# Scores of two head pairs in one tick, and the last norm's operands loaded at the end: a hybrid decoder layer

## The chip, the cores and the metric

The kernel runs on one core of one Trainium2 chip. A core has five engines that work side by side: TensorE (PE; its weight loads are listed apart as PEld), VectorE (DVE), ScalarE (ACT), GpSimd (POOL) and SyncE (SP, which here only issues DMAs). The metric is device time in microseconds. A forecast is a time and the chances of faster, same or slower.

## What is computed

One layer, 256 tokens of width 2048, all in float32. A norm, one input projection, two groups of 16 heads of 64 (sliding-window attention with sinks and ALiBi, two key heads shared; forgetting attention, FoX, where a decay of the running sum of log f is added), a norm per group, an output projection, a norm and the residual; then a GeGLU channel mixer with a causal convolution of width 3 and again a norm and the residual.

```python
h = rmsnorm(x, pre_mix_g); proj = h @ w_in
o_a = swa_sink_attention(q_a, k_a, v_a, sinks)      # 16 heads, window 128, ALiBi
o_b = forgetting_attention(q_b, k_b, v_b, log_f)    # 16 heads
mix = concat(rmsnorm(o_a, grp_swa_g), rmsnorm(o_b, grp_fox_g)) @ w_out
x = x + rmsnorm(mix, post_mix_g)
u = causal_dwconv(rmsnorm(x, pre_ffn_g) @ w_up, conv_w, conv_b)
y = (gelu(gate(u)) * val(u)) @ w_down
out = x + rmsnorm(y, post_ffn_g)
```

## The kernel before, in words

**Products.** Every weight tile is split into a high part (`whi`, a cast on ScalarE) and a low part (`wlo`, raw minus high, on VectorE; lines 112 and 115 for the projections), and each product is done as high x high, high x low and low x high. Each part has five buffers, so ScalarE and VectorE can be some units ahead of TensorE, and each raw tile too, filled by SP.

**Ticks.** TensorE's instructions run in the order in which the code issues them. The projections call `tick()` at fixed places: eight times in one `proj_T` (256 output columns, 32 products of 512 columns and 32 of 256), behind three of four k-tiles in the V projection, once per six products in the output projection. `later(n, f)` has `f` issued at the n-th tick from now. In this way attention work is dropped between the products of the projections. ScalarE, VectorE, GpSimd and SP get their order from a scheduler during the attention; in the last stage it is the order of the code.

**Attention.** Heads go in pairs, and a group is two pairs whose q (for FoX also k) comes from one projection. `attend` registers four steps per pair: `tables` (GpSimd writes the bias table into tile `p`, two buffers; for FoX after a DMA of `cb`), `scores` (12 products on 64 rows each, line 475, into two banks of the ring "att", which has four; then on VectorE four passes of line 481 that add the table and take the maximum, on ScalarE four exponentials of line 493, on VectorE the reciprocal 497 and four scalings 500), `transposes` (six of `p`, line 510, into two banks, then split) and `pv` (the weighted values, lines 522 to 536, into one bank, then into `oT`). `stages(n)` gives the ticks of the last three: n, n + 6, n + 9; the tables come three ticks before n. Sliding-window pairs take n = 6 and 14 after their group's start, FoX pairs n = 3 and 11, in groups of 16 ticks. FoX keys are scaled on GpSimd (line 442) and split into `keys` (lines 312 and 313) before their scores.

**The end.** The down projection goes in two halves of 22 tiles of 128 hidden features, each in two column passes, with `sums` (of the tag "x") as an operand of the fast products. In the last pass the products of the last three units are held back for the end (`block(i)`), their weights being read from `rest`. Then for each token half: the sum of the last banks (`down`, 1097 and 1098, with the squares on ScalarE), times the gain vector `gbf` on GpSimd (`gain`, 1091), the rstd (`rstd_y`, a power on GpSimd, 1173), and `finish` (1177: y times rstd plus `x_back` on VectorE, and the store). GpSimd's order there is: gain of four 512-wide pieces, the rstd of the first token half, three and a half more, the second rstd, the last half piece. `gbf` is loaded when the second half's up projection is over; the two halves of `x_back` are loaded into `tb` and `extra`, buffers of the weight loads, when each is free.

Of the kernel before, what the change touches and what calls it, by code (L numbers as in the profile page):

```python
# [17 lines left out]
P = 128  # L18
S = 256
D = 2048  # L20
# [11 lines left out]
def hybrid_layer(ctx: ExitStack, tc: tile.TileContext, x, pre_mix_g, w_in, b_forget, sinks,  # L32
# [27 lines left out]
    def later(n, f):  # L60
        todo.setdefault(now[0] + n, []).append(f)
# [253 lines left out]
    with tc.tile_pool(name="mixp", bufs=1) as mp:  # L315
# [277 lines left out]

        def stages(n):
            return n, n + 6, n + 9

# [23 lines left out]
        for g in range(4):  # L620
            if g == 0:
                b2 = bq0
            else:
                b2 = [bank(), bank()]
                proj_T(w_in, g * 256, b2)
            for m in range(2):
                swa_pair(2 * g + m, q_pair(b2[m]), stages(6 + 8 * (2 * g + m) - 8 * g))

# [59 lines left out]
        for g in range(4):  # L688
            bq = [bank(), bank()]
            proj_T(w_in, 1280 + g * 256, bq)  # L690
            qs = [q_pair(b) for b in bq]
            bk = [bank(), bank()]
            proj_T(w_in, 2304 + g * 256, bk)
            for m in range(2):
                ki = (2 * g + m + 2) % NK
                k_pair(bk[m], ki)
                fox_pair(2 * g + m, qs[m], ki, stages(3 + 8 * m))


        later(stages(11)[2] + 4, lambda: group_rstd(1, rstd_b))  # L700
        mix_sb = main.tile([P, 2, D], F32, tag="y", name="mix_sb")
# [145 lines left out]
    with tc.tile_pool(name="ffn", bufs=1) as fp:  # L847
# [200 lines left out]
        ysq = [small.tile([P, 5], F32, tag=f"ysq{t}", bufs=1, name=f"ysq{t}") for t in range(2)]  # L1048
        gbf = None
        for half in range(2):  # L1050
# [4 lines left out]
            for g in range(FHALF // 2):  # L1055
# [32 lines left out]
            def gain(t, n, h=None, into=None):  # L1088
                cs = slice(0, 512) if h is None else slice(h * 256, h * 256 + 256)
                ys = y_sb[:, t, n * 512:(n + 1) * 512][:, cs]  # L1090
                pool.tensor_tensor(ys if into is None else into, ys,
                                   gbf[:, n * 512:(n + 1) * 512][:, cs], op=ALU.mult)

# [19 lines left out]
            for n in (0, 2):  # L1113
# [39 lines left out]
                for i in range(4):  # L1153
                    block(i)
                    t, c = divmod(i, 2)
                    if half:
                        down(t, n + c, late[i])
                    else:
                        dve.tensor_tensor(y_of(t, c), late[i], y_of(t, c), op=ALU.add)

        def before_last(t, n):
# [14 lines left out]
        def finish(t, cs, r, q, y=None):  # L1176
            dve.scalar_tensor_tensor(y_sb[:, t, cs], y_sb[:, t, cs] if y is None else y, r,
                                     x_back[t][:, cs], op0=ALU.mult, op1=ALU.add)
            q.dma_start(of[t * P:(t + 1) * P, cs], y_sb[:, t, cs])
# [3 lines left out]
                     mybir.EngineType.SP}))  # L1183
        x_back = [tb[:, 0:2, :].rearrange("p a c -> p (a c)"),
                  extra.rearrange("p a c -> p (a c)")]
        for t in range(2):
            sp.dma_start(x_back[t], x_dram[t * P:(t + 1) * P, :])
        gain(0, 0)
# [61 lines left out]
```

## Time and profile before

| | us |
|---|---|
| median of 3 runs | 1069.38 (1068.11 to 1071.11) |
| the profiled execution, its own time | 1067.23 |
| its span in the trace | 1065.5 |
| TensorE busy in the span | 1051.2 |
| VectorE, ScalarE, GpSimd busy | 843.8, 637.6, 225.9 |

The granted clock is 0.997 on average. Rows of the trace give the start in us from the span's beginning, the duration in us, engine, line, operation, written tile <- read tiles, shapes, a count and, in brackets, the idle time ahead and what ended it. "x2" behind a row means that two are merged into it. A busy TensorE may still go slowly: spacings of its products tell that.

### The profile page before, as it was taken

How to read it: one execution, taken by the hardware profiler on the slowest of the kernel's cores; microseconds unless marked ns; L12 is line 12 of the kernel's file. 1: busy time of each engine (PE TensorE's matmuls, PEld its weight loads, DVE VectorE, ACT ScalarE, POOL GpSimd, SP SyncE). 2: the span in 40 equal slices, each digit the busy share in tenths (PEclk: the TensorE clock that was granted, in tenths of full speed). 3: DMA queues.
4: the chain of work that ended last, by engine and by line, in shares of the span. 5: the costliest groups of instructions: out<-in, count | busy, mean ns of one | idle time of the engine just before them, and what ended most of it. 6: DMA issues, size and time to landing. Idle time of an engine off the chain costs nothing.

```text
span 1065.5 us, 16294 instructions
## 1 busy us (share of the span) xinstructions
PE 1051.2 (99%) x5890; PEld 913.3 (86%) x5890; DVE 843.8 (79%) x1369; ACT 637.6 (60%) x1096; POOL 225.9 (21%) x256
## 2 busy tenths in 40 slices
PE   9999999999999999999999999999999999999996
PEld 7889988887889988888888888888888888888885
DVE  5988877887567888687777989668778687789996
ACT  6766766666656766565555555446566565656561
POOL 4243343342022121121212000002112121200103
PEclk9999999999999999999999999999999999999998
DMA  8745656555783776665666565666566665666572
GB/s 289 209 119 171 180 164 205 170 150 158 294 259 106 257 225 190 198 196 165 214 182 195 181 225 191 223 189 192 181 198 196 192 188 182 196 215 206 188 250 86
DMA packets 154284, 207.08 MB, mean 194 GB/s; under 512 B 6844, under 2 KB 131036, under 8 KB 153180
## 3 DMA queue, kind: packets, MB, share of 16 engines
q1 hardware_dynamic: 153200, 203.37, 61.0%
q10 hardware_dynamic: 1004, 2.68, 0.6%
q8 instruction: 46, 0.75, 0.3%
q14 instruction: 34, 0.28, 0.1%
HBM read 201.68 MB, written 4.21 MB: 193 GB/s over the span
## 4 chain that ended last, share of the span: by engine, by line
PE 91%; DVE 4%; DMA 1%; POOL 1%; issue 1%; ACT 1%; SPq 0%; DVEq 0%; POOLq 0%; ACTq 0%
PE bank_acc L284 16%; PE bank_att L967 15%; PE bank_att L284 14%; PE bank_acc L309 12%; PE bank_acc L290 8%; PE bank_att L290 7%; PE bank_acc L253 7%; PE bank_acc L258 3%; PE bank_acc L967 3%; PE bank_att L475 1%; PE bank_att L510 1%; DVE wlo L115 1%; DVE wlo L313 1%; PE bank_acc L932 1%; DMA x_in<-in_x_dram 1%
## 5 line engine op out<-in xcount | busy, mean ns | idle before, releaser
L115 DVE TENSOR_TENSOR wlo<-raw,whi 128x1024 fp32r<-128x1024 f32 (+3 forms) x271 | 330.3, 1229 | 117.4 <-ACT whi L112 112.9
L112 ACT CAST whi<-raw 128x1024 fp32r<-128x1024 f32 (+3 forms) x270 | 273.3, 1029 | 124.8 <-issue 88.9
L899 POOL TENSOR_TENSOR room<-room,rowf 128x256 f32<-128x256 f32 x88 | 100.3, 1160 | 393.9 <-DVE room L898 392.0
L284 PE MATMUL bank_acc<-hT,whi 128*128 128x512 f32 x736 | 173.3, 390 | 0.0
L284 PEld LDWEIGHTS bank_acc<-hT,whi 128*128 128x128 f32 x736 | 136.4, 188 | 27.4
L967 PE MATMUL bank_att<-whi,G 128*128 128x512 f32 x488 | 156.1, 389 | 0.0
L284 PE MATMUL bank_att<-hT,whi 128*128 128x512 f32 x640 | 150.6, 390 | 0.0
L284 PEld LDWEIGHTS bank_att<-hT,whi 128*128 128x128 f32 x640 | 118.7, 188 | 23.9
L967 PEld LDWEIGHTS bank_att<-whi,G 128*128 128x128 f32 x488 | 91.6, 188 | 18.9
L967 PE MATMUL bank_att<-wlo,G 128*128 128x512 f32 x244 | 95.0, 389 | 0.4 <-DVE wlo L313 0.4
L290 PEld LDWEIGHTS bank_acc<-hT,wlo 128*128 128x128 f32 x736 | 89.3, 188 | 2.0
L290 PE MATMUL bank_acc<-hT,wlo 128*128 128x256 f32 x736 | 89.9, 279 | 0.0
L901 ACT ACTIVATE room<-room,cw 128x256 f32<-128x256 f32 x88 | 53.0, 602 | 60.6 <-POOL room L899 60.6
L253 PE MATMUL bank_acc<-hT,whi 128*128 128x512 f32 x352 | 89.2, 396 | 0.0
L309 PE MATMUL bank_acc<-whi,oT 128*128 128x512 f32 (+1 forms) x272 | 82.5, 380 | 0.0
L290 PEld LDWEIGHTS bank_att<-hT,wlo 128*128 128x128 f32 x640 | 77.6, 188 | 1.7
L290 PE MATMUL bank_att<-hT,wlo 128*128 128x256 f32 x640 | 77.9, 279 | 0.0
L903 DVE SCALAR_TENSOR_TENSOR room<-room,cw 128x256 f32<-128x256 f32 x88 | 62.4, 709 | 17.6 <-ACT room L901 17.3
L253 PEld LDWEIGHTS bank_acc<-hT,whi 128*128 128x128 f32 x352 | 63.0, 188 | 11.3
L313 DVE TENSOR_TENSOR wlo<-raw,whi 128x1024 fp32r<-128x1024 f32 (+1 forms) x56 | 61.3, 1118 | 13.4 <-ACT whi L312 13.4
L312 ACT CAST whi<-tb 128x1024 fp32r<-128x1024 f32 x42 | 44.0, 1050 | 43.4 <-PE bank_att L967 19.7
L312 ACT CAST whi<-raw 128x1024 fp32r<-128x1024 f32 (+1 forms) x56 | 52.4, 958 | 28.9 <-PE bank_att L967 22.3
(255 smaller groups left out, 1591.1 us busy)
## 6 DMA issues: line engine op xcount, KB each, us to landing
raw<-in_w_up_dram SPq DMA_DIRECT2D x176, 512.0 KB, 4.1
raw<-in_w_down_dram SPq DMA_DIRECT2D x58, 512.0 KB, 4.9
raw<-in_w_in_dram SPq DMA_DIRECT2D x51, 512.0 KB, 3.9
raw<-in_w_out_dram SPq DMA_DIRECT2D x32, 512.0 KB, 4.3
extra<-in_w_down_dram SPq DMA_DIRECT2D x20, 512.0 KB, 4.8
raw<-in_w_in_dram SPq DMA_DIRECT2D x16, 384.0 KB, 3.5
tb<-in_w_down_dram SPq DMA_DIRECT2D x10, 512.0 KB, 3.6
cb<-c_dram SPq DMA_DIRECT2D x8, 256.0 KB, 3.6
```

The source lines that it names most:

```text
L112: i1 = act.copy(hi[:, cs], raw[:, cs])
L115: i2 = dve.tensor_tensor(lo[:, cs], raw[:, cs], hi[:, cs].bitcast(F32), op=ALU.subtract)
L253: pe.matmul(b, parts[u][0][:, a, m * P:(m + 1) * P], hT[:, kt, :], start=(kt == 0), stop=(kt == KT - 1))
L284: pe.matmul(b, parts[u][0][:, a, m * P:(m + 1) * P], hT[:, kt, :], start=(kt == 0), stop=(kt == KT - 1))
L290: pe.matmul(b[:, 256:512], parts[u][1][:, a, m * P:(m + 1) * P], hT[:, kt, 0:256], start=False, stop=False)
L309: pe.matmul(b, a, r[:, cols], start=(first and i == 0), stop=(last and i == 2))
L312: act.copy(hi, src)
L313: dve.tensor_tensor(lo, src, hi.bitcast(F32), op=ALU.subtract)
L899: pool.tensor_tensor(u[:, 2:258], u[:, 2:258], rowf, op=ALU.mult)
L901: act.activation(y, u[:, 2:258], AF.Identity, bias=cw[:, 3, ch:ch + 1], scale=cw[:, 2, ch:ch + 1])
L903: dve.scalar_tensor_tensor(y, u[:, 1:257], cw[:, 1, ch:ch + 1], y, op0=ALU.mult, op1=ALU.add)
L967: pe.matmul(b[:, to] if to else b, a, r[:, cols], start=(first and i == 0), stop=(last and i == 2))
```

## The change

`stages` gets the pair's number m: both pairs of a group have their scores in one tick; the first keeps n, n + 6, n + 9, the second gets n, n + 9, n + 13. Sliding-window groups take n = 7 and FoX groups n = 6. `gbf` and `x_back` are allocated and loaded after all the weight loads: `x_back` as a tile of its own in the place of `sums`, `gbf` in the place of `extra`, and `rest` moves to the place of `hT`. The function `gain` moves, with the same content.

```diff
-        def stages(n):
-            return n, n + 6, n + 9
+        def stages(n, m):
+            return n, n + 6 + 3 * m, n + 9 + 4 * m
...
-                swa_pair(2 * g + m, q_pair(b2[m]), stages(6 + 8 * (2 * g + m) - 8 * g))
+                swa_pair(2 * g + m, q_pair(b2[m]), stages(7 + 8 * g, m))
...
-                fox_pair(2 * g + m, qs[m], ki, stages(3 + 8 * m))
+                fox_pair(2 * g + m, qs[m], ki, stages(6, m))
...
-        later(stages(11)[2] + 4, lambda: group_rstd(1, rstd_b))
+        later(stages(6, 1)[2] + 4, lambda: group_rstd(1, rstd_b))
...
-            if half == 1:
-                gbf = main.tile([P, 4 * D], F32, tag="hT", name="gbc_ffn")[:, 0:D]
-                sp.dma_start(gbf, post_ffn_g[0].partition_broadcast(P))
...
-                    rest = main.tile([P, 2, 2, UNIT], F32R, tag="x", name="rest")
+                    rest = main.tile([P, 2, 2, UNIT], F32R, tag="hT", name="rest")
...
-                                     x_back[t][:, cs], op0=ALU.mult, op1=ALU.add)
+                                     x_back[:, t, cs], op0=ALU.mult, op1=ALU.add)
...
-        x_back = [tb[:, 0:2, :].rearrange("p a c -> p (a c)"),
-                  extra.rearrange("p a c -> p (a c)")]
+        x_back = main.tile([P, 2, D], F32, tag="x", name="x_back")
         for t in range(2):
-            sp.dma_start(x_back[t], x_dram[t * P:(t + 1) * P, :])
+            sp.dma_start(x_back[:, t, :], x_dram[t * P:(t + 1) * P, :])
+        gbf = fp.tile([P, D], F32, tag="gbc", name="gbc_ffn")
+        sp.dma_start(gbf, post_ffn_g[0].partition_broadcast(P))
         gain(0, 0)
```

What this does to the order on the engines, at three places. TensorE at the scores of the first FoX group, before: one pair's twelve products stand among the low products (`wlo`) of the next q projection.

```order
L258 MATMUL bank_acc<-hT,wlo 128x256 x10
L475 MATMUL bank_att<-keys,qh 128x256 x2
L475 MATMUL bank_att<-keys,ql 128x256 x2
L475 MATMUL bank_att<-keys,qh 128x256 x2
L475 MATMUL bank_att<-keys,qh 128x128 x2
L475 MATMUL bank_att<-keys,ql 128x128 x2
L475 MATMUL bank_att<-keys,qh 128x128 x2
L258 MATMUL bank_acc<-hT,wlo 128x256 x6
L253 MATMUL bank_acc<-hT,whi 128x512 x16
```

TensorE at the same place in the changed kernel, from the first pair's last three rows on (its first three and the product rows ahead, `L253` x14, are left out): the second pair follows at once, and 2 high and 16 low products of the two units in use come behind.

```order
L475 MATMUL bank_att<-keys,qh 128x128 x2
L475 MATMUL bank_att<-keys,ql 128x128 x2
L475 MATMUL bank_att<-keys,qh 128x128 x2
L475 MATMUL bank_att<-keys,qh 128x256 x2
L475 MATMUL bank_att<-keys,ql 128x256 x2
L475 MATMUL bank_att<-keys,qh 128x256 x2
L475 MATMUL bank_att<-keys,qh 128x128 x2
L475 MATMUL bank_att<-keys,ql 128x128 x2
L475 MATMUL bank_att<-keys,qh 128x128 x2
L253 MATMUL bank_acc<-hT,whi 128x512 x2
L258 MATMUL bank_acc<-hT,wlo 128x256 x16
L253 MATMUL bank_acc<-hT,whi 128x512 x16
```

So the block has moved behind 6 low and 14 high products, and two blocks have become one. VectorE at the scores of the second FoX group (`p_2340` is the first pair's table, `nm` the maxima, `rs` the sums), before:

```order
L481 ISA p_2340,nm_2382<-bank_att_2368,p_2340 128x256
L481 ISA nm_2382 128x1
L481 ISA p_2340,nm_2382<-bank_att_2369,p_2340 128x256
L481 ISA nm_2382 128x1
L481 ISA p_2340,nm_2382<-bank_att_2368,p_2340 128x128
L481 ISA nm_2382 128x1
L481 ISA p_2340,nm_2382<-bank_att_2369,p_2340 128x128
L481 ISA nm_2382 128x1
L497 RECIPROCAL rs_2387<-rs_2387 128x4
L500 TENSOR_SCALAR p_2340<-p_2340,rs_2387 128x256 x2
L500 TENSOR_SCALAR p_2340<-p_2340,rs_2387 128x128 x2
L115 TENSOR_TENSOR wlo_2595<-raw_2592,whi_2594 128x1024
```

VectorE at that place in the changed kernel, behind the first pair's four passes (`p_2373`): the second pair's (`p_2383`) lie around the first pair's reciprocal and scaling, and then comes the next split.

```order
L481 ISA p_2383,nm_2468<-bank_att_2454,p_2383 128x256
L481 ISA nm_2468 128x1
L497 RECIPROCAL rs_2444<-rs_2444 128x4
L481 ISA p_2383,nm_2468<-bank_att_2455,p_2383 128x256
L481 ISA nm_2468 128x1
L500 TENSOR_SCALAR p_2373<-p_2373,rs_2444 128x256 x2
L500 TENSOR_SCALAR p_2373<-p_2373,rs_2444 128x128 x2
L481 ISA p_2383,nm_2468<-bank_att_2454,p_2383 128x128
L481 ISA nm_2468 128x1
L481 ISA p_2383,nm_2468<-bank_att_2455,p_2383 128x128
L481 ISA nm_2468 128x1
L115 TENSOR_TENSOR wlo_2586<-raw_2583,whi_2585 128x1024
```

So eight passes instead of four stand between two splits; ahead of them the splits `wlo_2522`, `wlo_2528` and `wlo_2580` are already done, and `wlo_2404` and `wlo_2410` are those in use. SP at the end, before:

```order
L69 DMA raw<-in_w_down_dram 128x1024 x3
L1187 DMA tb<-x_dram 128x2048
L69 DMA raw<-in_w_down_dram 128x1024
L1187 DMA extra<-x_dram 128x2048
L1179 DMA out_dram<-y_sb 128x512 x6
```

SP at the end in the changed kernel:

```order
L69 DMA raw<-in_w_down_dram 128x1024 x4
L1182 DMA x_back<-x_dram 128x2048 x2
L1184 DMA gbc_ffn<-in_post_ffn_g_dram 128x2048
L1175 DMA out_dram<-y_sb 128x512 x6
L1175 DMA out_dram<-y_sb 128x256
```

The last weight load no longer stands behind a load of x, and the gain vector comes third behind two of x, a megabyte each. GpSimd's order at the end stays as told above.

More of the change, by code (lines that the diff above doesn't have):

```diff
@@ L1048, in hybrid_layer @@
         ysq = [small.tile([P, 5], F32, tag=f"ysq{t}", bufs=1, name=f"ysq{t}") for t in range(2)]
-        gbf = None
         for half in range(2):
@@ L1083, in hybrid_layer @@
                     token_sums(sums[:, FAST.index(g), :], *ys)
-            if half == 1:
-                gbf = main.tile([P, 4 * D], F32, tag="hT", name="gbc_ffn")[:, 0:D]
-                sp.dma_start(gbf, post_ffn_g[0].partition_broadcast(P))
[L1088 to L1092, printed above, removed]
             def down(t, n, b, h=None):
@@ L1159, in hybrid_layer, with gain @@
                         dve.tensor_tensor(y_of(t, c), late[i], y_of(t, c), op=ALU.add)
+        def gain(t, n, h=None, into=None):
+            cs = slice(0, 512) if h is None else slice(h * 256, h * 256 + 256)
+            ys = y_sb[:, t, n * 512:(n + 1) * 512][:, cs]
+            pool.tensor_tensor(ys if into is None else into, ys,
+                               gbf[:, n * 512:(n + 1) * 512][:, cs], op=ALU.mult)
         def before_last(t, n):
```

## The prediction

> **What bounds the kernel.** I read the busy line of the page and the shares of the chain that ended last, then a table by stretch, then the order of time inside the stretches in which TensorE lost time.
>
> ```profile
> PE 1051.2 (99%) x5890; PEld 913.3 (86%) x5890; DVE 843.8 (79%) x1369; ACT 637.6 (60%) x1096; POOL 225.9 (21%) x256
> PE 91%; DVE 4%; DMA 1%; POOL 1%; issue 1%; ACT 1%; SPq 0%; DVEq 0%; POOLq 0%; ACTq 0%
> 150.00:175.00 25.00, 23.85 (x150) 20.59 (x148) 17.50 (x34) 14.05 (x28) 13.65 (x20) 1.00 0.64 203
> 225.00:250.00 25.00, 24.19 (x146) 20.37 (x145) 20.92 (x43) 15.23 (x37) 11.48 (x16) 1.00 0.53 150
> 1000.00:1050.00 50.00, 49.64 (x220) 40.73 (x219) 44.40 (x54) 26.91 (x33) 3.43 (x4) 1.00 0.53 179
> 1050.00:1065.50 15.50, 6.04 (x44) 5.56 (x42) 9.86 (x15) 1.74 (x6) 6.48 (x7) 0.81 0.37 135
> 363.81 3.63 PE bank_att L284 x16
> 367.44 3.73 PE bank_att L290 x32
> ```
>
> TensorE is the bound: 99% busy, 91% of the chain. (In the stretches the columns after the length are PE, PEld, DVE, ACT, POOL busy, then the granted clock, the DMA share and GB/s.) A 512-column product costs 3.63/16 = 0.227 us, a 256-column one 3.73/32 = 0.117 us, and the change adds or removes none. So the time can move only where TensorE stalls: 1.15 us in 150:175, 0.81 in 225:250, 0.36 in 1000:1050; in the seams of the score blocks, which count as busy; and in the tail after 1050, where VectorE and GpSimd set the end.
>
> **Part 1, scores three ticks later in the FoX groups.** The first and the last FoX score block stall for their keys:
>
> ```profile
> 158.94 1.33 PE L258 MATMUL bank_acc<-hT,wlo 128*128 128x256 f32 x10
> 161.41 0.39 PE L475 MATMUL bank_att<-keys,qh 64*128 64x256 f32 x2 [1.13 <-ACT keys L312]
> 162.53 0.73 PE L258 MATMUL bank_acc<-hT,wlo 128*128 128x256 f32 x4
> 162.07 0.43 DVE L313 TENSOR_TENSOR keys<-scr,keys 128x256 fp32r<-128x256 f32 x1 [0.19 <-ACT keys L312]
> 243.83 0.39 PE L475 MATMUL bank_att<-keys,qh 64*128 64x256 f32 x2
> 245.15 0.45 PE L475 MATMUL bank_att<-keys,qh 64*128 64x256 f32 x4 [0.81 <-DVE keys L313]
> 245.28 0.43 DVE L313 TENSOR_TENSOR keys<-scr,keys 128x256 fp32r<-128x256 f32 x1 [0.19 <-ACT keys L312]
> 245.75 0.50 PE L309 MATMUL bank_acc<-whi,oT 128*128 128x512 f32 x1
> ```
>
> The ten products from 158.94 end at 160.11, the seam below adds 0.09, so the block that starts at 161.41 is 1.2 late; it then takes 1.12 (to 162.53) where a free one takes 0.84: 1.5 lost. The block at 243.83 takes 1.92: 1.1 lost. The last keys of each are written at 162.50 and 245.71. In a projection the three ticks hold 14 products of 0.227 and 6 of 0.117, 3.9 us, so the first block moves to some 164.1; in the output projection a tick is 6 x 0.227 = 1.36 us, so the last moves from 243.8 to 247.9. These lie 1.6 and 2.2 us behind the keys, and I take the whole **2.6 us**. Nothing gained would mean keys as late as the move, which the work in front of them does not give: on GpSimd both tables of the first group stand ahead of the keys' scaling now as before.
>
> **Part 2, two score blocks become one, eight times.** A free block shows its seams:
>
> ```profile
> 173.21 1.32 PE L258 MATMUL bank_acc<-hT,wlo 128*128 128x256 f32 x10
> 174.46 0.39 PE L475 MATMUL bank_att<-keys,qh 64*128 64x256 f32 x2
> 174.69 0.28 PE L475 MATMUL bank_att<-keys,ql 64*128 64x256 f32 x2
> 174.81 0.34 PE L475 MATMUL bank_att<-keys,qh 64*128 64x256 f32 x4
> 174.98 0.28 PE L475 MATMUL bank_att<-keys,ql 64*128 64x128 f32 x2
> 175.09 0.28 PE L475 MATMUL bank_att<-keys,qh 64*128 64x128 f32 x2
> 175.30 0.99 PE L258 MATMUL bank_acc<-hT,wlo 128*128 128x256 f32 x6
> 176.12 0.63 PE L253 MATMUL bank_acc<-hT,whi 128*128 128x512 f32 x2
> ```
>
> Entering: ten products should take 1.17 and 174.46 - 173.21 is 1.25, so 0.08. Leaving: six should take 0.70 and took 0.82, so 0.12. Inside, the first pair of products takes 0.23 where the next takes 0.12, and the last 0.21 where the one ahead takes 0.11: 0.21 more. A merge saves the 0.20 of one entry and one exit for sure; if the second block also runs on without the slow first and last pair, 0.41. I take the middle, 0.30, since no trace here shows two blocks back to back: 8 x 0.30 = **2.4 us** (1.6 to 3.3).
>
> The Trainium skill (TensorEngine Tiling (Array Packing), Key Properties) says that a change of tiling mode drains TensorE; these blocks are the only 64-row ones. That rule speaks for the entry and the exit alone: by it the saving is 1.6 us and the total below 0.8 us smaller.
>
> Cover for part 2: VectorE now takes eight passes over the banks in a row, and the low-part splits queue behind them, with ScalarE's exponentials between.
>
> ```profile
> 176.50 0.41 DVE L481 CUSTOM_DVE_ANT_0 p<-bank_att,p 128x256 f32<-128x256 f32 x1
> 178.86 0.18 DVE L497 RECIPROCAL rs<-rs 128x4 f32<-128x4 f32 x1 [1.17 <-ACT p L493]
> 179.07 1.01 DVE L500 TENSOR_SCALAR p<-p,rs 128x256 f32<-128x256 f32 x4
> 180.00 1.22 DVE L115 TENSOR_TENSOR wlo<-raw,whi 128x1024 fp32r<-128x1024 f32 x1
> ```
>
> One pair holds VectorE from 176.50 to 180.00, 3.5 us. Two pairs in the new order: part of the second pair's passes fills the 1.17 us wait, the rest adds 0.76, so the next split starts after 4.3 and is done after 5.5. The order of the changed kernel has the splits of the two units in use and of three more ahead of the burst: TensorE has 2 + 16 + 16 products of 0.227 and 16 + 16 + 8 of 0.117 left, 12.4 us, before it needs the first split behind it. Cost 0 to TensorE; with one unit fewer ahead it would still be covered. The transposes of the first pair follow six ticks (8 to 10 us) after the scores, its probabilities are ready after about 4.5 to 6. All four "att" banks are taken in one tick; the last that held them, the previous second pair's output, is three ticks old. GpSimd, 13.65 of 25 us busy in its heaviest stretch here, gets its two tables in a row and has three ticks or more before VectorE reads them.
>
> **Part 3, the tail.** The gain vector's load leaves the start of the second half's down projection and becomes the third megabyte behind x on SP's queue, and x waits until TensorE has read the sums for the last time:
>
> ```profile
> 1033.66 0.39 PE L967 MATMUL bank_att<-whi,sums 128*128 128x512 f32 x1
> 1034.58 0.33 SPq L1187 DMA_DIRECT2D extra<-x_dram  x1
> 274.00:285.00 11.00, 11.00 (x53) 9.18 (x52) 5.16 (x8) 6.71 (x10) 1.81 (x3) 1.00 0.88 332
> 280.00:291.00 11.00, 11.00 (x52) 9.11 (x52) 4.03 (x6) 5.08 (x7) 1.07 (x2) 1.00 1.00 401
> 1035.00:1041.00 6.00, 6.00 (x28) 4.96 (x27) 5.96 (x7) 3.10 (x4) 0.00 (x0) 1.00 0.56 196
> 996.13 3.53 POOL L1091 TENSOR_TENSOR y_sb<-y_sb,gbc_ffn 128x512 f32<-128x512 f32 x2 [52.46 <-ACT junk L1098]
> 1045.13 2.89 POOL L1091 TENSOR_TENSOR y_sb<-y_sb,gbc_ffn 128x512 f32<-128x512 f32 x2 [45.47 <-ACT junk L1098]
> 1049.47 0.55 POOL L1173 TENSOR_TENSOR ry<-rv,mhalf 128x1 f32<-128x1 f32 x1 [1.44 <-DVE rv L1171]
> 1050.05 3.48 DVE L1177 SCALAR_TENSOR_TENSOR y_sb<-y_sb,ry,tb 128x512 f32<-128x512 f32 x2 [0.66 <-POOL ry L1173]
> ```
>
> x can be issued at 1034.1 on TensorE's clock. The x load issued at 1034.58 moved its bytes from about 1036, 1.3 us later, and was over by 1041 at 196 GB/s with half-empty engines. Three queued loads are 3.15 MB: at 401 GB/s (the full queue of 280:291) 7.9 us, landing at 1043.3; at 332 (274:285, where two such loads and the like vector of the mix norm went through) 9.5 us, landing at 1044.9; at 196, 16.1 us, landing at 1051.5. I take 332, the row with the same transfers. Then GpSimd multiplies four 512-wide pieces at 2.89/2 = 1.45 us and takes the power of the first rstd behind them in its queue: 1044.9 + 5.8 + 0.55 = 1051.25 against 1050.02 before, when two pieces were done at 999. VectorE's line L1177 waits for that rstd and all that follows on VectorE to the end (the second half's last sums, squares, rstd) is behind it. The tail grows by **1.2 us**: 0 at 401 GB/s, 7.8 at 196.
>
> The Trainium skill (DMA: Bandwidth & Descriptors, Specifications) gives about 358 GB/s of HBM per core and 0.6 us to the first byte: an estimate from that page lands the vector at 1043.5, and the tail would grow by nothing. The trace shows full queues on both sides of that rate, 332 and 401 GB/s.
>
> Moving the early gains away from 996 gives something back there:
>
> ```profile
> 996.42 2.08 DVE L313 TENSOR_TENSOR wlo<-tb,whi 128x1024 fp32r<-128x1024 f32 x1
> 1001.02 0.61 PE L967 MATMUL bank_att<-whi,G 128*128 128x512 f32 x2
> 1002.00 0.50 PE L967 MATMUL bank_att<-wlo,G 128*128 128x512 f32 x1 [0.36 <-DVE wlo L313]
> ```
>
> Beside those two gains a split took 2.08 us, not the 1.22 of the one at 180.00, and 5 us later TensorE waits for a split: its two products from 1001.02 end their turn at 1001.47, the next starts at 1002.00, 0.5 us late. I take **0.5 us** as regained (0 to 0.6). The weight loads that the vector no longer precedes, and the second operands ("rest") in another tile, touch no TensorE stall: 0, between 0.3 either way.
>
> **Sum.** -2.6 - 2.4 + 1.2 - 0.5 = -4.3 us. The profiled execution took 1067.23 (span 1065.5, 1.7 around it): 1062.9. The median of the runs is 1069.38, 2.15 above it; from the median, 1065.1. What this kernel's measurement can tell from no change is about 0.3%, 3.2 us.
>
> **Rivals.** (A) The forecast: -4.3, and -3 to -5.2 with the bounds of the merge and a tail of 0.3 to 2. Chance 0.50.
> (B) The vector lands late, at 1047 to 1048 (about 250 GB/s, between the rows), and the tail grows by 3.5 to 4.5 us, with a merge worth only its entry and exit: -0.5 to -2, so about 1068. For it: a lone megabyte ran at 196. Against it: queued ones ran at 332 and 401. Chance 0.26.
> (C) The vector lands in time and the merge saves all it can: -2.6 - 3.3 - 0.5 = -6.4, 1063.0. For it: the 401 row. Against it: the 332 of the row with the same transfers. Chance 0.15. (The Trainium skill's DMA page, above, is on this rival's side for the vector.)
> (D) Slower: the burst of two pairs on VectorE starves TensorE of low parts. If only the units in use were split ahead of the burst, the next would be needed after 1.5 (scores) + 0.45 + 0.94 us and be ready about 6.0 after the scores began: 3.1 us lost, eight times, 25 us, so 1090; it decides the sign from 0.5 us per burst on. Against it: VectorE is 79% busy, no stall for a split stands in 150 to 250 now, and the order above. A vector that lands after 1049 has the same sign. Chance 0.09.
>
> A gives faster 0.37 and same 0.13; B same 0.24, slower 0.02; C faster 0.15; D slower 0.07, same 0.02. Faster 0.52, same 0.39, slower 0.09. The range 1062.8 to 1069.6 holds A, B and C.
>
> **What would show it.** Right: TensorE busy 25.0 of 25 in the stretches of the first and last FoX scores; 24 score products from first to last in about 1.5 us with one slow entry; SP issues x at 1034 less what was gained, the vector lands some 11 us later, and GpSimd's four gains run in one go, ending about 1.2 us later against TensorE's last products than the rstd did before. Wrong: a wait of TensorE for wlo or for "p" after a score block; a gain that starts more than 13 us after the last use of the sums; a double block of 1.7 us or more.

## The result, and the profile after

The changed kernel took 1063.86 us in the median of 6 runs (1063.68 to 1065.01), the kernel before 1069.72 (1068.11 to 1071.68, 6 runs) beside it: a ratio of 0.9947, 95% interval 0.9934 to 0.996. Six more runs of it in a later session gave 1064.31 against 1068.59, ratio 0.9955 (0.9939 to 0.9971). So it is faster by about half a per cent; the forecast was 1065.1 and faster. Of all the runs in this document two, one of before (1762.12 us) and one of the kernel with the late gain vector (1306.71), went at granted clocks of 0.556 and 0.753 throughout and count in no ratio.

The busy line of the page of the changed kernel, and the same four stretches as before (columns: length, then PE, PEld, DVE, ACT, POOL busy, the granted clock, the DMA share, GB/s):

```profile
PE 1049.6 (99%) x5890; PEld 914.6 (86%) x5890; DVE 839.7 (79%) x1369; ACT 639.1 (60%) x1096; POOL 229.3 (22%) x256
150.00:175.00 25.00, 25.00 (x163) 21.91 (x162) 18.00 (x41) 16.11 (x34) 10.18 (x15) 1.00 0.66 205
225.00:250.00 25.00, 25.00 (x152) 21.49 (x151) 20.53 (x35) 16.04 (x31) 12.01 (x16) 1.00 0.50 154
1000.00:1050.00 50.00, 49.83 (x230) 41.32 (x229) 43.60 (x51) 22.72 (x28) 8.95 (x7) 1.00 0.53 191
1050.00:1062.60 12.60, 2.07 (x18) 1.86 (x16) 7.02 (x14) 1.74 (x6) 3.57 (x5) 0.70 0.44 161
```

TensorE is busy 25.00 of 25 in both stretches with the first and last FoX scores: the waits for keys are gone. A double block, in order of time:

```profile
218.92 0.61 PE L253 MATMUL bank_acc<-hT,whi 128*128 128x512 f32 x2
219.47 0.38 PE L475 MATMUL bank_att<-keys,qh 64*128 64x256 f32 x2
...
220.78 0.28 PE L475 MATMUL bank_att<-keys,qh 64*128 64x128 f32 x2
221.00 0.73 PE L253 MATMUL bank_acc<-hT,whi 128*128 128x512 f32 x2
221.57 0.86 PE L258 MATMUL bank_acc<-hT,wlo 128*128 128x256 f32 x6
```

Its 24 products take 221.00 - 219.47 = 1.53 us, and so do those of the other seven double blocks, within 0.01. With the seams (two 512-column products should take 0.454; they take 0.55 ahead and 0.57 behind) a double block costs 1.53 + 0.10 + 0.12 = 1.75. Two lone ones cost 2 x (0.08 + 0.84 + 0.12) = 2.08. One merge saves 0.33, eight save 2.6.

The list of TensorE's waits shows one new kind, and the order of time shows where (in the second trace of this kernel it has two of them, 0.8 us together, the longer 0.5). The last row is the one wait near 1030:

```profile
PE bank_att L522 <- DVE pl L313: 0.5, 1, 0.5
135.82 0.50 PE L522 MATMUL bank_att<-pl,vpa 128*128 128x512 f32 x1 [0.54 <-DVE pl L313]
134.75 1.01 DVE L313 TENSOR_TENSOR pl<-bank_att,ph 128x384 fp32r<-128x384 f32 x2
1029.98 0.50 PE L967 MATMUL bank_att<-wlo,G 128*128 128x512 f32 x1 [0.17 <-DVE wlo L313]
```

The weighted values of a windowed pair wait until VectorE has split the transposed probabilities. The transposes were over at 130.86; VectorE comes to their split (the row at 134.75) 3.9 us later, because the second pair's reciprocal and scalings, two weight splits and four operations of the next projection stand ahead of it. And the end:

```profile
1029.61 0.80 SPq L1182 DMA_DIRECT2D x_back<-x_dram  x2
1032.22 0.33 SPq L1184 DMA_DIRECT2D gbc_ffn<-in_post_ffn_g_dram  x1
1032.00:1038.00 6.00, 6.00 (x28) 4.98 (x27) 5.96 (x8) 2.66 (x3) 0.00 (x0) 1.00 1.02 426
1040.68 3.00 POOL L1154 TENSOR_TENSOR y_sb<-y_sb,gbc_ffn 128x512 f32<-128x512 f32 x2 [100.80 <-DMA gbc_ffn<-in_post_ffn_g_dram]
1043.96 2.54 POOL L1154 TENSOR_TENSOR y_sb<-y_sb,gbc_ffn 128x512 f32<-128x512 f32 x2 [0.28 <-ACT junk L1088]
1045.71 0.81 DVE L1167 SCALAR_TENSOR_TENSOR rv<-ysq,rv 128x1 f32<-128x1 f32 x1 [0.85 <-ACT junk L1088]
1046.59 0.55 POOL L1169 TENSOR_TENSOR ry<-rv,mhalf 128x1 f32<-128x1 f32 x1
1047.18 3.47 DVE L1173 SCALAR_TENSOR_TENSOR y_sb<-y_sb,ry,x_back 128x512 f32<-128x512 f32 x2 [0.66 <-POOL ry L1169]
```

The gain vector is issued 2.6 us behind x, when its buffer is free, and GpSimd takes it up at 1040.68, 11.07 us after x was issued. The transfers did not go at one rate: 168 GB/s from 1030 to 1032, 426 from 1032 to 1038 (the row of that stretch), 93 from 1038 to 1041. GpSimd's four gains end at 1046.50, the first token half's variance `rv` at 1046.52, and its rstd `ry` follows at 1046.59. From the start of that `ry` to the end of the span it is 16.0 us (15.97 to 16.09) in all fourteen traces, of both kernels and of the experiments below. So the end is set by what lets the first `ry` start.

### The profile page after: what moved, and what is told of

It reads as the page before. It is cut to its first block, busy times and chain, and to the rows that moved or that the text cites. A ratio compares the mean times of both kernels' runs of the same rounds, so it can differ in the third digit from the quotient of the medians.

```text
span 1062.6 us, 16272 instructions
## 1 busy us (share of the span) xinstructions
PE 1049.6 (99%) x5890; PEld 914.6 (86%) x5890; DVE 839.7 (79%) x1369; ACT 639.1 (60%) x1096; POOL 229.3 (22%) x256
## 4 chain that ended last, share of the span: by engine, by line
PE 84%; DVE 9%; issue 2%; DMA 2%; ACT 2%; POOL 1%; DVEq 0%; SPq 0%; POOLq 0%; ACTq 0%
PE bank_acc L284 15%; PE bank_att L284 14%; PE bank_acc L309 12%; PE bank_att L967 9%; PE bank_acc L290 8%; PE bank_att L290 7%; PE bank_acc L253 7%; DVE wlo L313 4%; PE bank_acc L258 4%; PE bank_acc L967 2%; PE bank_att L475 1%; PE bank_att L510 1%; DVE wlo L115 1%; PE bank_acc L932 1%; DMA raw<-in_w_down_dram 1%
## 5 line engine op out<-in xcount | busy, mean ns | idle before, releaser
L253 PE MATMUL bank_acc<-hT,whi 128*128 128x512 f32 x352 | 88.0, 395 | 0.0
L253 PEld LDWEIGHTS bank_acc<-hT,whi 128*128 128x128 f32 x352 | 63.3, 188 | 11.5
```

What stands on the lines that cost most here:

```text
L253: pe.matmul(b, parts[u][0][:, a, m * P:(m + 1) * P], hT[:, kt, :], start=(kt == 0), stop=(kt == KT - 1))
```

## Where the time went, by stretch

The start of the same product of TensorE (score, transpose and value products left out) is compared between a trace and the first trace of before. The change of that difference over a stretch is what TensorE gained or lost there; the last column is the time from the end of the last product to the end of the span, against the 9.48 us of before. "Start" is the execution's own difference at 39 us, ahead of everything that was edited. "Near 1000", from 985 to 1012, is where the last column pass of the down projection begins (the pass border). Within the rounding the five columns add up to the difference of the spans, but for the kernel with FoX 3 ticks later, which lost another 0.3 between 303 and 985.

| trace | start | 39 to 303 (attention) | near 1000 | near 1030 | tail |
|---|---|---|---|---|---|
| forecast | 0 | -5.0 | -0.5 | 0 | +1.2 |
| changed kernel | +0.9 | -4.7 | -0.7 | +0.5 | +1.0 |
| changed kernel, second trace | -0.1 | -4.4 | -0.7 | 0.0 | +1.6 |
| before, second trace | +1.0 | -0.1 | -0.2 | 0.0 | 0.0 |
| new ticks, old end | +0.3 | -4.4 | +0.5 | 0.0 | 0.0 |
| old ticks, new end | -0.5 | +0.9 | -0.7 | +0.2 | +1.5 |
| FoX 3 ticks later, nothing merged | +0.5 | -2.7 | +1.3 | 0.0 | 0.0 |
| merged at the old ticks | -0.5 | -3.1 | +3.1 | 0.0 | 0.0 |
| new ticks, old end, late gain vector | -0.1 | -4.7 | -0.4 | 0.0 | +0.4 |
| changed, `rest` and x exchanged | -0.2 | -4.3 | -0.6 | 0.0 | 0.0 |
| the same, gain vector in a free buffer | 0.0 | -4.3 | +0.3 | 0.0 | 0.0 |
| old ticks, that end | +0.5 | 0.0 | -0.6 | 0.0 | 0.0 |
| merged at the old ticks, that end | -0.1 | -3.1 | -0.7 | 0.0 | 0.0 |
| changed, exchanged, values a tick later | +0.5 | -5.1 | +0.5 | 0.0 | 0.0 |

## Experiments

The theory was the forecast's sum; the rivals were that the gain came from one of the two attention edits alone, and that the end gave nothing or took some back. The first four kernels take the change apart, beside 27 runs of before with a median of 1068.44.

**The ticks alone.** The attention of the changed kernel with the end of before.

```diff
 (before.py)
-            return n, n + 6, n + 9
+            return n, n + 6 + 3 * m, n + 9 + 4 * m
...
-                swa_pair(2 * g + m, q_pair(b2[m]), stages(6 + 8 * (2 * g + m) - 8 * g))
+                swa_pair(2 * g + m, q_pair(b2[m]), stages(7 + 8 * g, m))
...
-                fox_pair(2 * g + m, qs[m], ki, stages(3 + 8 * m))
+                fox_pair(2 * g + m, qs[m], ki, stages(6, m))
```

> The scores' part of the change alone (ticks as in the changed kernel; gain vector, x and rest loaded and placed as before). Theory: the score terms carry all of the gain. The key stalls of the first and last FoX group go (2.6 us) and eight merges save 0.34 each (2.75, the spacing in the changed kernel's trace), so -5.3 us, a ratio near 0.995; the end of this kernel looks like the end before. Rival: the change at the end carries a part (the median moved 5.9 us, twice what the two profiled executions differ by), then this kernel gains 3 us or less and the end alone the rest.

Measured: 1063.85 (5 runs), ratio 0.9965 (0.9951 to 0.9978). The attention gain of the changed kernel is there (4.4; the 5.3 expected did not count the waits for `pl`), and half a microsecond is lost near 1000. In order of time there, in this run:

```profile
975.29 0.69 DVE L1007 TENSOR_TENSOR tb<-extra 128x512 f32<-128x512 f32 x1 [1.34 <-DMA extra<-in_w_down_dram]
977.66 0.69 DVE L1008 TENSOR_TENSOR tb<-tb,extra 128x512 f32<-128x512 f32 x1 [0.55 <-DMA tb<-in_w_down_dram]
992.61 3.53 POOL L1091 TENSOR_TENSOR y_sb<-y_sb,gbc_ffn 128x512 f32<-128x512 f32 x2 [52.95 <-ACT junk L1098]
992.89 2.10 DVE L313 TENSOR_TENSOR wlo<-tb,whi 128x1024 fp32r<-128x1024 f32 x1
997.21 1.21 DVE L313 TENSOR_TENSOR wlo<-tb,whi 128x1024 fp32r<-128x1024 f32 x1
998.48 0.50 PE L967 MATMUL bank_att<-wlo,G 128*128 128x512 f32 x1 [0.85 <-DVE wlo L313]
```

VectorE waits for two weight loads near 975, then has no gap to the border; beside GpSimd's gains its split takes 2.10 us; TensorE waits 0.85 for a split that follows. More on this below.

**The end alone.** The changed kernel with the old four tick lines.

```diff
 (after.py)
-            return n, n + 6 + 3 * m, n + 9 + 4 * m
+            return n, n + 6, n + 9
...
-                swa_pair(2 * g + m, q_pair(b2[m]), stages(7 + 8 * g, m))
+                swa_pair(2 * g + m, q_pair(b2[m]), stages(6 + 8 * (2 * g + m) - 8 * g))
...
-                fox_pair(2 * g + m, qs[m], ki, stages(6, m))
+                fox_pair(2 * g + m, qs[m], ki, stages(3 + 8 * m))
```

> The end's part of the change alone (gain vector and x at the very end, rest in the place of hT; ticks as before). Theory: 0.7 us regained at 1001 (no gains of GpSimd beside VectorE there), 0.5 us lost at a new wait for a low part (the scheduler now splits rest ahead of it) and 0.5 us lost on the rstd behind late gains: +0.3 us, between -0.5 and +1. Rival: -2 to -3 us, because the weight loads are rid of the loads of x and of the vector. Both: the key stalls near 160 and 244 stay.

Measured: 1069.12 (11 runs), ratio 1.0006 (0.9997 to 1.0015). The end gains nothing: in this trace it wins 0.7 near 1000 and pays 1.7 at 1030 and in the tail, and the interval of the ratio holds no change. In this execution the wait for the first FoX keys was larger:

```profile
161.95 0.39 PE L475 MATMUL bank_att<-keys,qh 64*128 64x256 f32 x2 [2.15 <-ACT keys L312]
245.58 0.45 PE L475 MATMUL bank_att<-keys,qh 64*128 64x256 f32 x4 [0.70 <-DVE keys L313]
1045.00 2.99 POOL L1154 TENSOR_TENSOR y_sb<-y_sb,gbc_ffn 128x512 f32<-128x512 f32 x2 [100.90 <-DMA gbc_ffn<-in_post_ffn_g_dram]
1050.92 0.55 POOL L1169 TENSOR_TENSOR ry<-rv,mhalf 128x1 f32<-128x1 f32 x1
```

2.15 here, 1.13 in the trace of before: the price of the key waits is not the same each time. From the vector's landing to `ry` it is 5.92 us, as in the changed kernel (5.91).

**FoX three ticks later, nothing merged.**

```diff
 (before.py)
-                fox_pair(2 * g + m, qs[m], ki, stages(3 + 8 * m))
+                fox_pair(2 * g + m, qs[m], ki, stages(6 + 8 * m))
...
-        later(stages(11)[2] + 4, lambda: group_rstd(1, rstd_b))
+        later(stages(14)[2] + 4, lambda: group_rstd(1, rstd_b))
```

> Only the shift: both FoX pairs of a group three ticks later (6 and 14 instead of 3 and 11), nothing merged, sliding-window ticks and the end as before. Theory: the two key stalls go, -2.6 us, TensorE's score blocks still take 0.84 us plus 0.20 of seams each. Rival: the wait moves on to something else at the new ticks (tables or banks), 0 to -1 us.

Measured: 1065.75 (11 runs), ratio 0.9979 (0.9969 to 0.9988). The stretches of this run that had the key waits:

```profile
150.00:175.00 25.00, 25.00 (x155) 21.80 (x154) 18.46 (x33) 14.46 (x28) 11.86 (x16) 1.00 0.68 215
225.00:250.00 25.00, 25.00 (x150) 21.05 (x149) 19.58 (x40) 16.09 (x33) 13.47 (x16) 1.00 0.52 162
```

No wait is left and the attention gains 2.7 us, the 2.6 of the forecast's first part. In the traced execution 1.3 of it was lost near 1000.

**Both pairs in one tick, at the old ticks.**

```diff
 (before.py)
-            return n, n + 6, n + 9
+            return n, n + 6 + 3 * m, n + 9 + 4 * m
...
-                swa_pair(2 * g + m, q_pair(b2[m]), stages(6 + 8 * (2 * g + m) - 8 * g))
+                swa_pair(2 * g + m, q_pair(b2[m]), stages(6 + 8 * g, m))
...
-                fox_pair(2 * g + m, qs[m], ki, stages(3 + 8 * m))
+                fox_pair(2 * g + m, qs[m], ki, stages(3, m))
```

> Only the merge: both pairs of a group in one tick, but at the early ticks (3 in FoX, 6 in the sliding-window groups), the end as before. Theory: eight merges save 2.75 us; the key stalls stay in the first and last FoX group (2.6) and grow by up to 0.5 each, since the second pair's keys, split later, are now wanted in the same tick; the two FoX groups between had their keys 0.6 us ahead of the first pair's scores and may now wait some tenths: -1 to -2.5 us in all. Rival: the merge itself is worth nothing (seams paid elsewhere): 0 or slower.

Measured: 1065.37 (11 runs), ratio 0.9974 (0.9965 to 0.9983). That is more than the 1 to 2.5 us expected, because most of the key waits went too. The attention gains 3.1, against 4.4 in the second trace of the changed kernel. Two blocks make up the 1.2 between them, within 0.2: the first windowed one takes 2.43 us in place of 1.53 (it needs all four "att" banks one tick after the transposed gain columns took one, and waits until VectorE has copied these, the first row below), and the first FoX one 1.83. Waits for `pl` are in both (the second row; 0.57 here, 0.75 there). So the seventh tick of the windowed pairs is what the first block needs, and with the pairs merged FoX's three ticks are worth the 0.3 of its first block.

```profile
43.22 0.38 PE L475 MATMUL bank_att<-keys,qh 64*128 64x256 f32 x1 [0.52 <-DVE gcol L410]
58.49 0.50 PE L522 MATMUL bank_att<-pl,vpa 128*128 128x512 f32 x1 [0.57 <-DVE pl L313]
```

The next two rows are GpSimd's order of time in before, the one behind them is that of this run:

```profile
159.50 0.74 POOL L553 TENSOR_TENSOR sqs<-sqs,sqo 128x256 f32<-128x256 f32 x1
160.19 1.41 POOL L442 TENSOR_TENSOR scr<-scr 128x256 f32<-128x256 f32 x2
```

```profile
158.77 1.43 POOL L442 TENSOR_TENSOR scr<-scr 128x256 f32<-128x256 f32 x2
```

In before GpSimd scales the keys only behind an addition of squares (L553, 0.7 us) from an earlier pair; the later fourth step of that pair takes it out of the way, the tables ahead of it are over 0.7 us sooner as well, and the scaling begins 1.4 us sooner. Of the first key wait about 0.3 us is left. The last FoX group has another reason: there GpSimd waits for VectorE's product of the keys (L441), which stands at 237.83 here and at 241.91 in before, and the keys are split at 241.91, ahead of the block at 242.68.

**A second trace of before.** The same text as before.

> The kernel before, unchanged, for a second trace of it. Theory (its key waits near 160 and 244 are there each time, its stall at the pass border near 1000 varies with the execution): key stalls of 0.9 to 2.3 us, border stall anywhere from 0.5 to 3 us. Rival (the border stall is fixed by the program): 0.6 us again, as in the first trace.

Measured: 1067.91 (one run), span 1066.2, key waits of 1.13 and 0.84, a border wait of 0.16, less than either side expected. The startup was 1.0 us later than in the first trace, as it was by 0.9 in the first trace of the changed kernel: that much the same kernel differs by in one execution.

**The gain vector late, nothing else of the end.** Beside 11 runs of before, median 1068.47 (also for the two kernels after it).

```diff
 (new ticks, old end)
                 gbf = main.tile([P, 4 * D], F32, tag="hT", name="gbc_ffn")[:, 0:D]
-                sp.dma_start(gbf, post_ffn_g[0].partition_broadcast(P))
...
             sp.dma_start(x_back[t], x_dram[t * P:(t + 1) * P, :])
+        sp.dma_start(gbf, post_ffn_g[0].partition_broadcast(P))
```

> Attention of the changed kernel and the end of before, except that the gain vector is loaded behind the two halves of x instead of early; tiles of x and of the last cross products stay as in before. Theory (GpSimd's first gains beside VectorE are what makes the stall at the pass border near 1000): that stall, 1.0 us in the run with the score ticks alone, is under 0.2 us, VectorE's order at 1030 is before's (no new wait there), and the gains run near 1040; span about 1 us under that run's 1062.0, so a median near 1062.9, plus up to 0.5 if the late gains still slow the tail. Rival (the stall at the border comes from the order in which the last weights load, not from the gains): the stall stays at 0.5 to 1.9 us and the median stays at 1063.8 or above.

Measured: 1062.39 (5 runs), ratio 0.9945 (0.993 to 0.9959), span 1060.7. The wait near 1000 is gone, though VectorE had waited longer for its loads (1.83 + 0.54 us) than in the run with the early vector (1.34 + 0.55), and the vector landed at 1039.10 with a first `ry` at 1044.69:

```profile
974.97 0.69 DVE L1007 TENSOR_TENSOR tb<-extra 128x512 f32<-128x512 f32 x1 [1.83 <-DMA extra<-in_w_down_dram]
977.34 0.69 DVE L1008 TENSOR_TENSOR tb<-tb,extra 128x512 f32<-128x512 f32 x1 [0.54 <-DMA tb<-in_w_down_dram]
992.56 1.21 DVE L313 TENSOR_TENSOR wlo<-tb,whi 128x1024 fp32r<-128x1024 f32 x1
995.50 1.21 DVE L313 TENSOR_TENSOR wlo<-tb,whi 128x1024 fp32r<-128x1024 f32 x1
1039.10 5.50 POOL L1090 TENSOR_TENSOR y_sb<-y_sb,gbc_ffn 128x512 f32<-128x512 f32 x4 [100.25 <-DMA gbc_ffn<-in_post_ffn_g_dram]
```

From one of these splits to the next VectorE takes 995.50 - 992.56 = 2.94 us; with the gains beside it, 997.21 - 992.89 = 4.32. The lost 1.38 us is the cost of the early gains. The tail is 0.4 longer than before's, within the 0.5 expected: here too `ry` follows right behind the four late gains.

**`rest` and x exchanged.** `rest` back in the buffer of `sums`, x in that of `hT`.

```diff
 (after.py)
-                    rest = main.tile([P, 2, 2, UNIT], F32R, tag="hT", name="rest")
+                    rest = main.tile([P, 2, 2, UNIT], F32R, tag="x", name="rest")
...
-        x_back = main.tile([P, 2, D], F32, tag="x", name="x_back")
+        x_back = main.tile([P, 4, D], F32, tag="hT", name="x_back")
```

> The changed kernel with the tile of the last cross products (rest) back in the buffer that the sums leave, and x's in the one that the normed activations left; the gain vector's buffer as changed. Theory (rest in its own buffer is what let its splits go ahead of the last weight split on VectorE): the wait near 1030 for the low halves of the weights, 0.46 us more than before, is gone, VectorE's late chain ends about 2.8 us sooner, x is issued some us sooner than 1029.6 while the gain vector still waits for extra's split near 1032; median 1063.2 to 1063.5. Rival (the wait at 1030 is a matter of the last weights' DMA): it stays, median 1063.9.

Measured: 1062.54 (6 runs), ratio 0.9943 (0.9931 to 0.9955), span 1060.4. More than expected, and for another reason: x no longer waits for the sums, so it is loaded at 936, and the gain vector goes alone:

```profile
1029.52 0.33 SPq L1184 DMA_DIRECT2D gbc_ffn<-in_post_ffn_g_dram  x1
1035.28 2.99 POOL L1154 TENSOR_TENSOR y_sb<-y_sb,gbc_ffn 128x512 f32<-128x512 f32 x2 [96.09 <-DMA gbc_ffn<-in_post_ffn_g_dram]
1044.17 0.16 DVE L1167 SCALAR_TENSOR_TENSOR rv<-ysq,rv 128x1 f32<-128x1 f32 x1 [0.85 <-ACT junk L1088]
1044.41 0.55 POOL L1169 TENSOR_TENSOR ry<-rv,mhalf 128x1 f32<-128x1 f32 x1 [0.91 <-DVE rv L1167]
```

`rv` takes 0.16 again, GpSimd is idle 0.91 us ahead of `ry`, and `ry` stands 6.57 us ahead of the end of TensorE's last product, as in before, against 5.48 and 4.94 in the changed kernel. Here the tail is set by TensorE's products and not by the vector. The wait at 1030 is gone as well, but the second trace of the changed kernel has none either, so whether `rest` makes it stays open.

**The gain vector in that buffer too.**

```diff
 (the kernel above)
-        x_back = main.tile([P, 4, D], F32, tag="hT", name="x_back")
+        xg = main.tile([P, 4 * D], F32, tag="hT", name="xg")
+        x_back = xg[:, 0:2 * D].rearrange("p (t c) -> p t c", t=2)
...
-        gbf = fp.tile([P, D], F32, tag="gbc", name="gbc_ffn")
+        gbf = xg[:, 2 * D:3 * D]
```

> As the run before this one in the list, with the gain vector also in the buffer of the normed activations, so that no load of the end waits for a buffer. Theory (the tail's cost is that the gains run beside the last VectorE work, because the vector lands at 1040.7): it lands 5 to 10 us sooner, the gains are over before the last product ends, VectorE's last two-input operations take 1.4 us instead of 3.5, the tail behind the last product is 9.7 us again instead of 10.2, and with the wait at 1030 gone too the median is 1062.8 to 1063.2. Rival (earlier gains fall beside the splits of the last weights near 1026 to 1032 and slow these): a stall of 0.5 to 2 us of TensorE there, median 1063.8 to 1065.

Measured: 1063.18 (6 runs), ratio 0.9951 (0.9938 to 0.9964). The time and the short tail (that of before) are as expected, but not for the reason given: with no buffer to wait for, the vector was issued at 944 and not 5 to 10 us sooner, the first two gains ran at 992.07 again, a split took 2.09 us, and TensorE waited 0.67 us near 998. For the vector, waiting for a buffer is what puts it at the right time.

**Old ticks, and the merge at the old ticks, each with the end of the exchanged kernel; and the values a tick later.** These three ran beside 15 runs of before, median 1068.26. The first two are the exchanged kernel with the tick lines of before and with those of the merge at the old ticks; the third is the exchanged kernel with

```diff
-            return n, n + 6 + 3 * m, n + 9 + 4 * m
+            return n, n + 6 + 3 * m, n + 10 + 4 * m
```

> The tick numbers of before, with the end of the run that put the tile of the last cross products back. Theory (that end is worth 0.5 to 0.7 at the pass border near 1000 and 0.4 in the tail, whatever the ticks are): 1.1 us under the profiled execution of before, so about 1067.3 in the median of 1068.5, and more, up to 2, if the executions of before often stall longer at the border than their traces show. Rival (the end gains only together with the new ticks): no difference, 1068.5.

> Both head pairs' score products in one tick with FoX at its old tick 3 and the windowed pairs at 6, and the same end as the run before this one. Theory (the 3.1 us that this set of ticks gave back at the pass border near 1000 came from GpSimd's early gains): stall and slow products there are gone, span near 1061.3, median 1061.8 to 1062.4, within 0.6 of the run with ticks 6 and 7. Rival (the loss at the border came from where these ticks leave the queues): it stays, median 1064 or more.

> The run with the tile of the last cross products put back, and the fourth step of each pair (values times probabilities) one more tick later, 10 and 14 ticks behind the scores instead of 9 and 13. Theory (the new waits of TensorE near 58 and 135, 0.4 to 0.5 and 0.7 us, are for the split of the transposed probabilities, which VectorE does late): both are gone, 0.9 to 1.2 us less, median 1061.4. Rival (the step only meets other work a tick later, and the last group ends later): at most 0.3 either way, median 1062.5.

Measured: 1067.22 (11 runs), ratio 0.9991 (0.9982 to 1.0); 1063.67 (5 runs), 0.9953 (0.9941 to 0.9966); 1063.1 (5 runs), 0.9943 (0.9929 to 0.9956). The first: the median is 1.0 us lower, as expected, with an interval that reaches no change; its trace shows 0.6 of it near 1000 and nothing in the tail. The second: the 3.1 us near 1000 are gone, so its span is 3.2 us shorter than that of the same ticks with the old end; it stays behind the exchanged kernel's by 1.3, of which the first windowed block and the first FoX block make 1.2 (2.42 and 1.83 us in place of 1.53), which I had not allowed for. The third: the waits for `pl` are gone and the attention gains 5.1 instead of 4.3, though one score block (at 190.99) now takes 1.95 us; yet the median is no better. In its trace TensorE waits near 998 although no gain runs there:

```profile
976.70 0.69 DVE L1007 TENSOR_TENSOR tb<-extra 128x512 f32<-128x512 f32 x1 [3.30 <-DMA extra<-in_w_down_dram]
997.87 0.50 PE L967 MATMUL bank_att<-wlo,G 128*128 128x512 f32 x1 [0.63 <-DVE wlo L313]
```

This shows what the wait near 1000 is made of. VectorE waits for the weight loads near 976 and runs without a gap from there to the border; every tenth by which the load is late shows at the border, above a slack that the early gains shorten. VectorE's idle time for the two loads near 976, and TensorE's wait near 1000, by the rows of each trace:

| trace | idle for the loads | early gains | TensorE's wait |
|---|---|---|---|
| before, second trace | 1.15 | yes | 0.16 |
| before | 1.49 | yes | 0.36 |
| vector in a free buffer | 1.70 | yes | 0.67 |
| new ticks, old end | 1.89 | yes | 0.85 |
| FoX later, not merged | 2.74 | yes | 1.61 |
| merged at the old ticks | 2.88 | yes | 1.78 |
| the seven others without early gains | 1.66 to 2.37 | no | 0 |
| values a tick later | 3.30 | no | 0.63 |

With the early gains the wait is the idle time less 1.0 to 1.1; without them, less 2.7 by the one trace that has a wait. So the late vector gives 1.6 us of slack at this place, and what that is worth depends on how late the load comes in an execution. The two extreme rows of the upper part:

```profile
1002.70 0.50 PE L967 MATMUL bank_att<-wlo,G 128*128 128x512 f32 x1 [0.16 <-DVE wlo L313]
999.82 0.50 PE L967 MATMUL bank_att<-wlo,G 128*128 128x512 f32 x1 [1.78 <-DVE wlo L313]
```

The load is not issued late. In every trace VectorE's wait for the `extra` tile is 3.4 us shorter than the time from the load's issue to the end of the wait, and this time goes from 4.57 to 6.71 us. Two traces of one kernel differ in it by 0.33 us (before) and 0.72 (changed kernel); whether all of the spread comes from the execution, or some from the edits, was not tried.

**A second trace of the changed kernel.** The same text as after.

> The changed kernel once more, for a second trace and so that its ratio stands on as many runs as the others. Theory (it pays 0.5 at 1030 and 0.9 in the tail against the kernel with the cross products' tile put back): span 1.0 to 2.0 above that kernel's 1060.4, median 1063.5 to 1064.3, ratio near 0.996; the wait at 1030 for the low halves of the weights is there again. Rival (these two differ by the execution alone): no wait at 1030 and a tail of 9.5, ratio 0.9943 like that kernel's.

Measured: 1064.31 (6 runs), ratio 0.9955 (0.9939 to 0.9971), span 1062.0. The wait at 1030 is not there, the tail is 11.0 us: neither the theory nor the rival as I wrote them. The vector landed at 1040.13, the first `ry` began at 1046.05, 5.92 later:

```profile
1028.99 0.80 SPq L1182 DMA_DIRECT2D x_back<-x_dram  x2
1040.13 2.99 POOL L1154 TENSOR_TENSOR y_sb<-y_sb,gbc_ffn 128x512 f32<-128x512 f32 x2 [100.87 <-DMA gbc_ffn<-in_post_ffn_g_dram]
1046.05 0.55 POOL L1169 TENSOR_TENSOR ry<-rv,mhalf 128x1 f32<-128x1 f32 x1
```

From the landing to the end of the span it is 21.9 us in both traces of this kernel and 22.0 in the one with the old ticks. The vector sets the end; a small wait of TensorE at 1030 only moves its last product nearer to an end that stands fixed. The two columns near 1030 and tail belong together: +1.5, +1.6 and +1.7 in those three traces.

The shortest times are those of the kernel with `rest` and x exchanged and of the one with the late gain vector (1062.39). The six runs of the former, 1062.07 to 1063.11, all lie below all twelve of the changed kernel, 1063.19 to 1065.01. These were different sessions, with medians of before of 1068.47 there and of 1069.72 and 1068.59 here; the intervals of the ratios overlap, so that it beats the changed kernel is likely and not shown.

## Why the prediction was right, point by point

- **Keys, 2.6 us.** Right in size: 2.7 with the shift alone. What it did not see is that the merge by itself takes nearly all of this away, because it gives the keys an earlier place on GpSimd and VectorE. The sum counted the waits once, so it was not hurt.
- **Merges, 2.4 us.** 0.33 each by the rows above, 2.6 in all, against 0.30 taken as the middle of 0.20 and 0.41. 0.20 of it is the entry and the exit, so 0.13 of the 0.21 for the slow first and last pair is saved as well.
- **VectorE's burst, cost 0.** This is the step that failed, by 0.5 us in one trace and 0.8 in the other. No wait for a weight split followed a score block, and rival D with its 25 us has nothing for it. But VectorE's order also holds the splits of the transposed probabilities, and up to two of these came late, behind the second pair's work, for the values of windowed pairs. One tick more for the values removes both, which shows the cause. 2.6 + 2.6 - 0.8 = 4.4 us is what the table has for most traces with these ticks (4.3 to 4.7).
- **The tail, +1.2 us.** Right in mechanism, too small by 0.3 to 0.5: the cost was 1.5 to 1.7 us. The vector was there 11.07 and 11.14 us after x was issued (10.8 forecast), and the gains took 5.9 us to the rstd (5.8). That 332 GB/s fits is partly luck. With the forecast's 1.3 us ahead of the first bytes the mean rate is 322, but the queue went at 426 for six microseconds, above the 401 of rival C; a slow start and a slow end, for which the sum has no term, took the rest. Nor does it have the 2.6 us for which the vector waited for its buffer; they cost nothing, since x kept the queue full. Rival B needed a landing two to three microseconds later, C one without effect; neither happened.
- **The gains away from 996, -0.5 us.** -0.7 in both traces. Its size depends on how late the loads come, as the table of waits shows: with the early gains TensorE waited 0.16 to 1.78 us, without them not at all until the loads were 2.7 us late.
- **The sum, -4.3 us** on the profiled execution: the spans differ by 2.9, with a startup that was 0.9 later in that execution; without the startup -3.9, and -3.5 in the second trace. From the medians it is -5.9 in the first session and -4.3 in the second. The medians of before were 1068.26 to 1069.72 from session to session, so the 1.2 us between forecast and result is not more than that. By the time alone the 1063.0 of rival C is as near as the forecast; it is the rows, with 0.33 for a merge and a tail that grows, that speak for A.
- **Two sums of the rivals** do not come out of their terms: A's bounds give -2.7 to -6.1 and not -3 to -5.2, B's -0.2 to -1.2 and not -0.5 to -2. The forecast does not rest on them.

The two edits together gave what the ticks alone gave (1063.85 with the old end, 1063.86 and 1064.31 with the new): against the old end, the end's gain near 1000 (1.2 us) and its cost at 1030 and in the tail (1.5 and 1.6) nearly cancel.

## What to carry to other kernels

A transfer that is moved to the end has a right time with two edges: late enough that its consumer doesn't run beside an engine that has no slack, early enough that it isn't the last to land; find the chain of fixed length at the end (16.0 us here) and ask what starts it. When steps are moved on TensorE, follow every small operation that was between them on the other engines: here the place of the keys' scaling on GpSimd decided 1.4 us, and that of two splits on VectorE up to 0.8. And read the idle time of the feeding engine some 20 us ahead of a wait, not only the wait itself: here it told the size of the wait within 0.1 us wherever the early gains ran.

## What the runs showed of the hardware

A VectorE operation of 128 x 1 elements took 0.81 us in place of 0.16 when it fell beside GpSimd's gains, and ended at 1046.52, just behind the gain that ended at 1046.50; a split of 128 x 1024 took 2.10 in place of 1.21. The small operation was not slowed in proportion to its size but held until GpSimd was through; in the second trace of the changed kernel and in the one with the late vector it too ended 0.02 us behind a gain. The Trainium skill (SBUF — State Buffer, SBUF: two separate sides) has this as a rule: the two engines share a port pair that one holds for a whole instruction while the other blocks. The traces agree.

A load of the same weights, issued at the same place of the program, was waited for between 1.15 and 3.30 us from one trace to another, and the startup differed by 1.0 us for the same kernel. Differences of single traces below that are not to be put down to an edit unless a row shows their place.
